# Weight sums of the mixers moved into the second gate/up loops, head sums and projection loads shifted, a second transpose bank

## The chip, the cores and the metric

The program runs on one core of a Trainium2 chip. Time is device time in microseconds of one execution. The core has engines that run side by side, each through its own list of instructions in order: TensorE (PE, the matmuls), VectorE (DVE), ScalarE (ACT), GpSimd (POOL), and SyncE (SP), which issues the DMA transfers. An instruction that waits holds up all those behind it on its engine.

## The reference

A decoder trunk of two layers on x of shape (1, 1024, 1024), in float32:

```python
for layer in range(2):
    h = h + 0.5 * rmsnorm(swiglu(rmsnorm(h, g0), w_gate, w_up, w_down), g1)     # FFN 0
    m = rmsnorm(h, mix_pre_g[layer])
    m = hybrid_mixer(m, ...) if layer == 0 else stick_breaking(m, ...)
    h = h + rmsnorm(m, mix_post_g[layer])
    h = h + 0.5 * rmsnorm(swiglu(rmsnorm(h, g2), w_gate, w_up, w_down), g3)     # FFN 1

def swiglu(x, wg, wu, wd):
    return (silu(x @ wg) * (x @ wu)) @ wd            # 1024 -> 1408 -> 1024
```

The hybrid mixer projects h once, gives the parts to four heads of differential softmax attention (the difference of two softmax maps, blocks of 128 queries) and four heads of gated linear attention (GLA, chunks of 64), and projects the joined heads with `w_out`. Stick breaking is causal attention with eight heads whose weights come from sums of log(1 − sigmoid), with its own `w_out`.

## The kernel before

**Products.** Every float32 product is made of three passes over a high and a low part (`mm3`, L280 to L284). A raw weight tile is split by a cast on ACT (L331) and a subtraction on VectorE (L332) into a tile `wq` (helper `split_w`); the other operand, `hl`, is split in L272 and L273. Large products are done by Strassen-like schemes, which need sums and differences of weight blocks and save matmuls.

**Raw weights.** All weights come from DRAM into the pool `rp`, whose slots (tag `raw`) hold 512 KB each. There are four, given out in turn. A new load goes into the slot whose turn it is, once the last reader of what lay there is through. Gate, up, block, head and projection tiles all share these four.

**FFN** (`ffn`, L585). The function `gu` has two loops over the 11 columns (of 128) of gate and up. The first loop (from L398) takes one gate tile per column and does two quarters of 12 matmuls each (bank `pa`). It runs first in the program for FFN 0 of layer 0, right after the start. The second loop (from L425) takes a gate and an up tile per column, and makes on POOL four subtractions of blocks, in place:

```python
gt(out=b11, in0=b12, in1=b11, op=ALU.subtract)   # L431
gt(out=t2, in0=b22, in1=b11, op=ALU.subtract)    # L432
gt(out=b12, in0=b22, in1=b12, op=ALU.subtract)   # L433
gt(out=b21, in0=b21, in1=t2, op=ALU.subtract)    # L434
```

Five quarters of 12 matmuls follow, in the order t2 (bank `pb`), b12 (`pc`), b11 (`pd`), b21 (`pc` again, added on top) and b22 (`pd` again). VectorE takes the partial results out: `ph<-pb` (L444), `c22<-pc` (L447), `c22<-pd` (L461), `c21<-pc` (L464), `c12<-pd` (L467), and multiplies (L468, L469). So the second use of `pc` can only begin when `c22<-pc` has read the first. The splits into `wq` are one column ahead of the matmuls. From column 6 on, two more operations on POOL (`down_sums`, L608 and L609) prepare the down projection, `down_strassen`.

**Weight sums of the mixers.** The value projections and the output projections of both mixers use block sums too (`Blocks.sums`, L75). One job loads four blocks of 256 KB into two raw slots (`rawd`, L60), makes four subtractions on POOL (L64), and stores two results of 512 KB to DRAM (`vsum` or `wsum`, L87), from where the projection loads them later. There are 16 jobs: four for the hybrid mixer's value projection, in the first loop of the first FFN; eight (its output projection, and the value projection of layer 1) in the diff heads, at query blocks 1, 4 and 6; four (output projection of layer 1) in stick-breaking heads 0 to 3, at block 6.

**Heads.** Both kinds of attention run through `heads` (L978): per step one block of 128 queries of one head: scores (bank `z`), weights, transposes of the weights into the bank `tps` (L971) and copies from it (`att`, L973), the product with v (`po`), and a normalisation for which POOL makes `rs` (L230) and VectorE `on` (L1150). `self.soon` holds functions that run one step later, `steps` a list of projection steps of which one runs per block; at block 2 the steps for the next head are added (`fill`). Each projection step list loads its raw weights (`rawt`, L875) and splits them at its first step. `put_o` (L1414) stores a finished head (`otd`), loads two stored heads back (`raws`), makes sums of them on POOL a step later (`out_sums`, L1440 to L1443) and stores these (`osum`, L1429).

**Order.** The functions are written out in one thread; a scheduler then orders instructions on each engine, on SP too, by when it expects operands. Instructions that are kept in program order stay where they were written against each other.

Of the kernel before, what the change touches and what calls it, by code (L numbers as in the profile page):

```python
# [19 lines left out]
P = 128  # L20
D = 1024
# [23 lines left out]

class Blocks:
# [18 lines left out]

    def b11(self, j):
        return self.load((j, 0))[:, 0]

    def b21(self, j):
        return self.load((j + self.KH, 0))[:, 0]  # L70

    def b22(self, j):
        return self.load((j + self.KH, 1))[:, 0]

    def sums(self, j, dst):  # L75
# [5 lines left out]
        def make():  # L81
# [15 lines left out]
class Trunk:  # L97
# [247 lines left out]
    def gu(self, cx, wg, wu, A, xn1, gname, gi, jobs):  # L345
# [52 lines left out]
        for c in range(NF):  # L398
# [26 lines left out]
        for c in range(NF):  # L425
# [8 lines left out]
            gt(out=b21, in0=b21, in1=t2, op=ALU.subtract)  # L434
            pb = self.acc.tile([P, TB], F32, name="pb", tag="acc")
# [34 lines left out]
            if c > NF // 2:  # L470
                self.down_sums(ph, c - 1 - NF // 2)
        tmp.close()
# [112 lines left out]
    def ffn(self, l, f, x0, xn1, hsrc, hdst, last):  # L585
# [5 lines left out]
        jobs = [(self.value_blocks(0), j, self.tv) for j in range(4)] if l + f == 0 else []  # L591
# [281 lines left out]
    def load_tile(self, w, c0, n=P):  # L873
        r = self.rp.tile([P, KD, P], F32, name="rawt", tag="raw")
        self.nc.sync.dma_start(out=r[:, :, :n], in_=w[:, c0:c0 + n].rearrange("(k p) m -> p k m", p=P))  # L875
        return r

    def split_tile(self, w, c0, n=P):
        nc = self.nc
        r = self.load_tile(w, c0, n)  # L880
        wh = self.wp.tile([P, KD, P], F32R, name="wh", tag="w")
        wl = self.wp.tile([P, KD, P], F32R, name="wl", tag="w")
        nc.scalar.copy(out=wh[:, :, :n], in_=r[:, :, :n])
        nc.vector.tensor_tensor(out=wl[:, :, :n], in0=r[:, :, :n], in1=wh[:, :, :n].bitcast(F32), op=ALU.subtract)
        return wh, wl

    def proj_steps(self, w, c0, X, dst):

        wt = []

        def step(tb, kh):
            if not wt:
                wt.extend(self.split_tile(w, c0))
# [8 lines left out]
        return [lambda tb=tb, kh=kh: step(tb, kh) for tb in range(2) for kh in range(2)]  # L902

    def halves_first(self, a, b):
        return a[:2] + b[:2] + a[2:] + b[2:]
# [746 lines left out]
```

## Time and profile before

| | us |
|---|---|
| median of 3 runs | 2520.13 (2518.27 to 2523.79) |
| the profiled execution | 2520.03 |
| its span, first to last instruction | 2518.3 |
| TensorE busy | 2367.1 |
| VectorE busy | 1905.4 |
| ScalarE busy | 1139.0 |
| GpSimd busy | 889.1 |

The mean granted clock of TensorE is 0.983. Times in the trace count from the start of the span. The stages that matter here: first gate/up loop of the first FFN from 16.7 to 103.6 us, its second loop up to some 250; GLA in 510 to 660; the diff heads in 675 to 900; the stick-breaking heads in 1700 to 2125. A row of a timeline gives start, duration, engine, line, operation, output and inputs, and in brackets how long the engine was idle before it and what it waited for. A row of a group gives count, busy time, mean of one in ns, and the idle time before with its causes.

### The profile page before, as it was taken

What the parts mean: (1) busy time and instruction counts of PE and PEld (TensorE: products, weight loads), DVE (VectorE), ACT (ScalarE), POOL (GpSimd) and SP (SyncE); (2) the same over time, 40 slices, a digit from 0 to 9 for tenths busy, and PEclk for the clock granted to TensorE, in tenths of its full rate; (3) what the DMA queues carried; (4) which work ended last, traced back from release to release, by engine and by line L of the source; (5) the groups of instructions that cost most, each with busy time, mean ns of one, the idle gap of its engine ahead of it and who ended that gap; (6) DMA issues with size and microseconds to landing.
All of it is one profiled execution on the core that took longest, in us unless ns stands there. A gap on an engine that the chain in (4) does not pass through costs nothing.

```text
span 2518.3 us, 32043 instructions
## 1 busy us (share of the span) xinstructions
PE 2367.1 (94%) x11165; PEld 1926.7 (77%) x11165; DVE 1905.4 (76%) x2884; ACT 1139.0 (45%) x2286; POOL 889.1 (35%) x756
## 2 busy tenths in 40 slices
PE   6999998998988999999989999999999989999998
PEld 4788777777776777788868888777888877788886
DVE  5867888387576877768888678985666678786798
ACT  5423456332465756423456224563333335652343
POOL 4345532024123111545532456301322340244554
PEclk9999999999999999999999999999999999999999
DMA  7422544514325354222652225546220136622255
GB/s 242 118 83 68 185 158 141 167 51 147 113 95 174 129 199 141 76 84 78 212 177 82 84 71 171 164 150 217 84 84 26 59 109 225 194 84 75 71 167 193
DMA packets 272506, 324.27 MB, mean 129 GB/s; under 512 B 13828, under 2 KB 190168, under 8 KB 272344
## 3 DMA queue, kind: packets, MB, share of 16 engines
q1 hardware_dynamic: 272344, 322.22, 40.2%
q8 instruction: 88, 1.44, 0.2%
q14 instruction: 74, 0.61, 0.1%
HBM read 256.11 MB, written 66.06 MB: 128 GB/s over the span
## 4 chain that ended last, share of the span: by engine, by line
PE 35%; DVE 12%; issue 10%; DMA 6%; POOL 5%; ACT 2%; SPq 0%; POOLq 0%; DVEq 0%; ACTq 0%
DVE hl L273 4%; PE pc L283 2%; PE pc L284 2%; PE pc L282 2%; PE pd L283 2%; PE pd L284 2%; PE pd L282 2%; PE pa L284 2%; PE pa L282 2%; PE pa L283 2%; DMA rawd<-in_ffn_w_down_dram 1%; POOL rs L230 1%; PE pb L283 1%; PE pb L282 1%; PE pb L284 1%
## 5 line engine op out<-in xcount | busy, mean ns | idle before, releaser
L331 ACT CAST wq<-rawt 128x512 fp32r<-128x512 f32 x264 | 162.7, 623 | 364.5 <-PE pc L284 170.4
L230 POOL TENSOR_TENSOR rs<-ms,nhalf 128x1 f32<-128x1 f32 (+1 forms) x136 | 104.3, 774 | 498.8 <-DVE ms L228 382.1
L332 DVE TENSOR_TENSOR wq<-rawt,wq 128x512 fp32r<-128x512 f32 x264 | 247.0, 941 | 35.0 <-ACT wq L331 29.4
L282 PE MATMUL pps<-hl,wh 128*128 128x512 f32 x512 | 209.2, 409 | 2.1 <-DVE q L921 2.1
L431 POOL TENSOR_TENSOR rawt<-rawt 128x512 f32<-128x512 f32 x44 | 73.2, 1664 | 373.6 <-DMA rawt<-in_ffn_w_up_dram 240.9
L284 PE MATMUL pps<-hl,wl 128*128 128x512 f32 x512 | 204.1, 399 | 0.0
L283 PE MATMUL pps<-hl,wh 128*128 128x512 f32 x512 | 203.8, 398 | 0.0
L272 ACT CAST hl<-rawd 128x512 fp32r<-128x512 f32 x192 | 117.9, 620 | 150.9 <-PE dc L284 21.6
L273 DVE TENSOR_TENSOR hl<-rawd,hl 128x512 fp32r<-128x512 f32 x192 | 156.4, 819 | 28.0 <-ACT hl L272 27.5
L282 PE MATMUL pa<-hl,wq 128*128 128x512 f32 x352 | 144.8, 411 | 14.7 <-ACT ph L404 8.1
L284 PE MATMUL pa<-hl,wq 128*128 128x512 f32 x352 | 142.8, 406 | 12.0 <-DVE wq L332 12.0
L64 POOL TENSOR_TENSOR rawd<-rawd 128x512 f32<-128x512 f32 x64 | 88.9, 1390 | 157.0 <-DMA rawd<-in_sb_w_out_dram 100.8
L283 PE MATMUL pa<-hl,wq 128*128 128x512 f32 x352 | 142.0, 403 | 0.0
L273 DVE TENSOR_TENSOR hl<-ph,hl 128x512 fp32r<-128x512 f32 x136 | 141.6, 1053 | 0.0
L282 PE MATMUL pc<-hl,wq 128*128 128x512 f32 x336 | 131.4, 391 | 3.4 <-DVE c L447 3.4
L284 PE MATMUL pc<-hl,wq 128*128 128x512 f32 x336 | 132.1, 393 | 0.0
L283 PE MATMUL pc<-hl,wq 128*128 128x512 f32 x336 | 132.1, 393 | 0.0
L283 PE MATMUL pd<-hl,wq 128*128 128x512 f32 x336 | 131.3, 391 | 0.0
L284 PE MATMUL pd<-hl,wq 128*128 128x512 f32 x336 | 131.2, 390 | 0.0
L282 PE MATMUL pd<-hl,wq 128*128 128x512 f32 x336 | 131.0, 390 | 0.0
L1042 DVE TENSOR_TENSOR_SCAN a<-a,zero 128x128 f32<-128x128 f32 (+3 forms) x64 | 92.6, 1447 | 50.6 <-POOL a L1039 50.0
L955 PE MATMUL z<-k,q 128*128 128x512 f32 (+2 forms) x480 | 115.9, 365 | 2.7 <-ACT e L1114 2.6
(346 smaller groups left out, 6831.1 us busy)
## 6 DMA issues: line engine op xcount, KB each, us to landing
rawt<-in_ffn_w_gate_dram SPq DMA_DIRECT2D x88, 512.0 KB, 4.0
rawd<-in_ffn_w_down_dram SPq DMA_DIRECT2D x60, 512.0 KB, 4.0
rawd<-in_ffn_w_down_dram SPq DMA_DIRECT2D x116, 256.0 KB, 2.8
rawt<-in_ffn_w_up_dram SPq DMA_DIRECT2D x44, 512.0 KB, 4.0
hres<-h SPq DMA_DIRECT2D x40, 512.0 KB, 2.8
h<-hres SPq DMA_DIRECT2D x40, 512.0 KB, 4.5
vsum<-rawd SPq DMA_DIRECT2D x16, 512.0 KB, 2.8
rawd<-vsum SPq DMA_DIRECT2D x32, 256.0 KB, 3.4
```

Source lines behind the costliest of these rows:

```text
L64: self.t.nc.gpsimd.tensor_tensor(out=out, in0=a, in1=b, op=ALU.subtract)
L230: nc.gpsimd.tensor_tensor(out=rs, in0=ms, in1=self.nhalf.to_broadcast([P, n]) if n > 1 else self.nhalf, op=ALU.pow)
L272: nc.scalar.copy(out=t[:, 0], in_=src)
L273: nc.vector.tensor_tensor(out=t[:, 1], in0=src, in1=t[:, 0].bitcast(F32), op=ALU.subtract)
L282: nc.tensor.matmul(ps, lhsT=ah, rhs=bh, start=first, stop=False, skip_group_check=more)
L283: nc.tensor.matmul(ps, lhsT=ah, rhs=bl, start=False, stop=False, skip_group_check=more)
L284: nc.tensor.matmul(ps, lhsT=al, rhs=bh, start=False, stop=last, skip_group_check=more)
L331: nc.scalar.copy(out=w[:, 0], in_=src)
L332: nc.vector.tensor_tensor(out=w[:, 1], in0=src, in1=w[:, 0].bitcast(F32), op=ALU.subtract)
L431: gt(out=b11, in0=b12, in1=b11, op=ALU.subtract)
L955: nc.tensor.matmul(z[:, :wide], lhsT=lhs[:, i * P:(i + 1) * P], rhs=rhs[:, c0:c0 + wide], start=j == 0, stop=j == len(passes) - 1 and not ...
L1042: nc.vector.tensor_tensor_scan(out=ra, data0=ra, data1=self.zero1.to_broadcast([P, n]), initial=1.0, op0=ALU.mult, op1=ALU.add)
```

## The change

1. No job runs in the first loop, the diff heads or the stick-breaking heads any more. All are in second gate/up loops: eight (value and output projection of layer 0) in FFN 0 of layer 0, in columns 0 to 7; four (value projection of layer 1) in FFN 1 of layer 0; four (output projection of layer 1) in FFN 0 of layer 1. A job's blocks are loaded at the end of a column's code, its sums come behind the next column's four subtractions, its stores at that column's end. Loads and stores of jobs are kept in program order.
2. `put_o`: sums one step later as before, the stores another step later, kept in program order; in layer 1 the head at hand is used as it lies, not loaded again.
3. Projections of the heads behind the first: raw weights are loaded at block 1 (kept in program order), split at block 2 by `prep`; of two step lists that are interleaved, the second is split with the first one's first step.
4. Diff heads 0 to 2 have two transpose banks and one bank for the projections' accumulators; for head 3 the banks are opened again as before (one and two).

```diff
 class Blocks:
     def load(self, *places):
         r = self.t.rp.tile([P, 2, TB], F32, name="rawd", tag="raw")
         for i, (k, c) in enumerate(places):
-            self.t.nc.sync.dma_start(out=r[:, i], in_=self.src(k, c))
+            self.t.tc.keep_in_program_order(self.t.nc.sync.dma_start(out=r[:, i], in_=self.src(k, c)))
...
             self.sub(b[:, 0], b[:, 0], b[:, 1])
+            return store
+
+        def store():
             for i, t in enumerate((r, b)):
-                self.t.nc.sync.dma_start(out=dst[j][:, i * D:(i + 1) * D], in_=t.rearrange("p c m -> p (c m)"))
+                self.t.tc.keep_in_program_order(self.t.nc.sync.dma_start(
+                    out=dst[j][:, i * D:(i + 1) * D], in_=t.rearrange("p c m -> p (c m)")))
...
@@ first loop of gu
                 combos(c - 4)
-            if sums:
-                sums.pop(0)()
-            if jobs:
-                B, j, dst = jobs.pop(0)
-                sums.append(B.sums(j, dst))
@@ second loop of gu
             gt(out=b21, in0=b21, in1=t2, op=ALU.subtract)
+            sums = [f() for f in sums]
...
                 self.down_sums(ph, c - 1 - NF // 2)
+            if sums:
+                sums.pop(0)()
+            if jobs:
+                B, j, dst = jobs.pop(0)
+                sums.append(B.sums(j, dst))
@@ ffn
-        jobs = [(self.value_blocks(0), j, self.tv) for j in range(4)] if l + f == 0 else []
+        jobs = []
+        if l + f == 0:
+            jobs += [(self.value_blocks(0), j, self.tv) for j in range(4)]
+            jobs += [(self.out_blocks(0), j, self.td) for j in range(4)]
+        elif f != l:
+            jobs += [(self.value_blocks(1), j, self.tv) if f else (self.out_blocks(1), j, self.td) for j in range(4)]
@@ proj_steps
+        raw = [self.load_tile(w, c0, pin=True)] if early else []
         wt = []
+        def prep():
+            wt.extend(self.split_tile(w, c0, raw))
@@ halves_first
-        return a[:2] + b[:2] + a[2:] + b[2:]
+        def first():
+            a[0]()
+            b.prep()
+        return Steps([first, a[1]] + b[:2] + a[2:] + b[2:], a.prep)
@@ heads
-            job = weights(h, i) if u < n else None
-            if job:
-                self.soon.append(job)
...
+            if u < n and i == 1:
+                nxt = fill(h)
             if u < n and i == 2:
-                steps += fill(h)
+                nxt.prep()
+                steps += nxt
@@ diff heads
-                self.open_mix(pd, 4, 1, 1)
+                self.open_mix(pd, 4, 2, 1)
...
                 def start(h):
+                    if h == 3:
+                        pd.close()
+                        self.mctx.close()
+                        self.open_mix(pd, 4, 1, 1)
...
-                def weights(h, i):
-                    if jobs and i in (1, 4, 6):
-                        B, j, dst = jobs.pop(0)
-                        return B.sums(j, dst)
@@ put_o
-            r, o = [self.rp.tile([P, S], F32, name="raws", tag="raw") for _ in range(2)]
-            for t, m in ((r, self.out_order(l)[j]), (o, k)):
-                self.nc.sync.dma_start(out=t, in_=self.ot[l][m])
+            pin = self.tc.keep_in_program_order
+            r = self.rp.tile([P, S], F32, name="raws", tag="raw")
+            pin(self.nc.sync.dma_start(out=r, in_=self.ot[l][self.out_order(l)[j]]))
+            o = ot
+            if l == 0:
+                o = self.rp.tile([P, S], F32, name="raws", tag="raw")
+                pin(self.nc.sync.dma_start(out=o, in_=self.ot[l][k]))
             def sums():
                 self.out_sums(r, o, o, self.nc.gpsimd.tensor_tensor)
+                return store
+            def store():
                 for i, t in enumerate((r, o)):
-                    self.nc.sync.dma_start(out=self.sd[j][:, i * S:(i + 1) * S], in_=t)
+                    pin(self.nc.sync.dma_start(out=self.sd[j][:, i * S:(i + 1) * S], in_=t))
```

The order of instructions at three places, before and after. First SP in the second loop of the first FFN; the numbers behind the names tell tiles apart. Before:

```order
L342 DMA rawt_1007<-in_ffn_w_gate_dram 128x8x128
L342 DMA rawt_1009<-in_ffn_w_up_dram 128x8x128
L342 DMA rawt_1105<-in_ffn_w_gate_dram 128x8x128
L342 DMA rawt_1107<-in_ffn_w_up_dram 128x8x128
L342 DMA rawt_1203<-in_ffn_w_gate_dram 128x8x128
L342 DMA rawt_1205<-in_ffn_w_up_dram 128x8x128
```

After:

```order
L68 DMA rawd_1069<-in_hyb_w_in_dram 128x512 x2
L68 DMA rawd_1072<-in_hyb_w_in_dram 128x512 x2
L345 DMA rawt_1075<-in_ffn_w_gate_dram 128x8x128
L345 DMA rawt_1077<-in_ffn_w_up_dram 128x8x128
L89 DMA vsum1_133<-rawd_1069 128x1024
L89 DMA vsum1_133<-rawd_1072 128x1024
L68 DMA rawd_1179<-in_hyb_w_in_dram 128x512 x2
L68 DMA rawd_1182<-in_hyb_w_in_dram 128x512 x2
L345 DMA rawt_1185<-in_ffn_w_gate_dram 128x8x128
L345 DMA rawt_1187<-in_ffn_w_up_dram 128x8x128
```

With four slots given out in turn, rawt_1185 and rawt_1187 take the places of rawt_1075 and rawt_1077, the column just ahead of them; before, rawt_1203 took the place of rawt_1007, two columns ahead.

Second, VectorE in the same loop, one column with the splits for the next. Before:

```order
L444 TENSOR_TENSOR ph_447<-pb,ph_447 128x512
L332 TENSOR_TENSOR wq<-rawt,wq 128x512
L447 TENSOR_TENSOR c_1246<-pc,ph_447 128x512
L332 TENSOR_TENSOR wq<-rawt,wq 128x512
L461 TENSOR_TENSOR c_1246<-pd,c_1246 128x512
L332 TENSOR_TENSOR wq<-rawt,wq 128x512
L464 TENSOR_TENSOR c_1263<-pc,ph_447 128x512
L332 TENSOR_TENSOR wq<-rawt,wq 128x512
L467 TENSOR_TENSOR c_1264<-pd,ph_447 128x512
L332 TENSOR_TENSOR wq<-t_1403,wq 128x512
L468 TENSOR_TENSOR ph_446<-ph_446,c_1264 128x512
L469 TENSOR_TENSOR ph_447<-c_1263,c_1246 128x512
```

After:

```order
L443 TENSOR_TENSOR ph_352<-pb,ph_352 128x512
L335 TENSOR_TENSOR wq<-t_1189,wq 128x512
L335 TENSOR_TENSOR wq<-rawt,wq 128x512
L446 TENSOR_TENSOR c_1122<-pc,ph_352 128x512
L335 TENSOR_TENSOR wq<-rawt,wq 128x512
L460 TENSOR_TENSOR c_1122<-pd,c_1122 128x512
L335 TENSOR_TENSOR wq<-rawt,wq 128x512
L463 TENSOR_TENSOR c_1139<-pc,ph_352 128x512
L335 TENSOR_TENSOR wq<-rawt,wq 128x512
L466 TENSOR_TENSOR c_1140<-pd,ph_352 128x512
L467 TENSOR_TENSOR ph_351<-ph_351,c_1140 128x512
L468 TENSOR_TENSOR ph_352<-c_1139,c_1122 128x512
```

The split of the next column's t2 moved from behind `c12<-pd` (two multiplications ahead of the next column) to behind the next column's `ph<-pb`, ahead of `c22<-pc`.

Third, POOL in the diff heads. Before:

```order
L64 TENSOR_TENSOR rawd<-rawd 128x512
L230 TENSOR_TENSOR rs<-ms,nhalf 128x1
L64 TENSOR_TENSOR rawd<-rawd 128x512 x2
L230 TENSOR_TENSOR rs<-ms,nhalf 128x1
L64 TENSOR_TENSOR rawd<-rawd 128x512 x6
L230 TENSOR_TENSOR rs<-ms,nhalf 128x1
L64 TENSOR_TENSOR rawd<-rawd 128x512 x3
L1440 TENSOR_TENSOR raws<-raws 128x512
L230 TENSOR_TENSOR rs<-ms,nhalf 128x1 x5
```

After:

```order
L233 TENSOR_TENSOR rs<-ms,nhalf 128x1 x7
L1468 TENSOR_TENSOR raws<-raws 128x512
L1469 TENSOR_TENSOR raws<-raws 128x512
L1470 TENSOR_TENSOR raws<-raws 128x512
L233 TENSOR_TENSOR rs<-ms,nhalf 128x1
```

The block subtractions (`rawd`) are gone from between the `rs`; those of the head sums (`raws`) stay.

More of the change, by code (lines that the diff above doesn't have):

```diff
@@ L43, in tile, with __init__ @@
         return self.pool().tile(shape, dtype, name=name, tag=self.tag)
+class Steps(list):
+    def __init__(self, steps, prep):
+        super().__init__(steps)
+        self.prep = prep
 class Blocks:
@@ L64, in sub @@
         self.t.nc.gpsimd.tensor_tensor(out=out, in0=a, in1=b, op=ALU.subtract)
[L66 to L73, printed above, removed]
     def sums(self, j, dst):
@@ L900, in step @@
                 dst(ps, slice(tb * TB, (tb + 1) * TB))
-        return [lambda tb=tb, kh=kh: step(tb, kh) for tb in range(2) for kh in range(2)]
+        return Steps([lambda tb=tb, kh=kh: step(tb, kh) for tb in range(2) for kh in range(2)], prep)
     def halves_first(self, a, b):
-        return a[:2] + b[:2] + a[2:] + b[2:]
+        def first():
+            a[0]()
+            b.prep()
+        return Steps([first, a[1]] + b[:2] + a[2:] + b[2:], a.prep)
     def scaled(self, t, scale):
@@ L976, in transposer, with heads @@
         return res, [lambda j0=j0: group(j0) for j0 in range(0, i + 1, 4)]
-    def heads(self, H, first, second, third, fill, start, weights, steps):
+    def heads(self, H, first, second, third, fill, start, steps):
         LAG = 2
@@ L1022, in heads @@
                 third(*done)
-        for step in steps + self.soon:
+        for step in steps:
             step()
+        while self.soon:
+            self.soon = [g for g in [f() for f in self.soon] if g]
     def sb_weights(self, q, k, i):
@@ L1087, in sb_mixer @@
             self.heads(8, lambda h, i: self.sb_weights(q[h], k[h], i), second, lambda h, i, r: None,
-                       lambda h: project(h + 1) if h < 7 else self.out_steps(1), start,
-                       lambda h, i: self.out_blocks(1).sums(h, self.td) if h < 4 and i == 6 else None, begin[5:])
+                       lambda h: project(h + 1) if h < 7 else self.out_steps(1), start, begin[5:])
             pd.close()
@@ L1406, in fill @@
                         return self.out_steps(0)
-                    return self.halves_first(q_diff(h + 1), k_diff(h + 1))
+                    return self.halves_first(q_diff(h + 1, True), k_diff(h + 1, True))
                 self.heads(4, lambda h, i: self.diff_weights(q[h], k[h], i, rcs),
                            lambda h, i, pts: self.diff_rows(rcs.pop(0), v[h // 2], (h % 2) * P, i, pts),
-                           third, fill, start, weights, begin[2:])
+                           third, fill, start, begin[2:])
                 pd.close()
@@ L1497, in out_steps @@
         self.begun = B, order, st
-        return [lambda tp=tp, ns=ns: step(tp, ns) for tp in range(2) for ns in ((0, 1), (2, 3), (4, 5), (6,))]
+        return Steps([lambda tp=tp, ns=ns: step(tp, ns) for tp in range(2) for ns in ((0, 1), (2, 3), (4, 5), (6,))],
+                     lambda: None)
     def mix_out(self, l, hsrc, hdst, gname, gi):
```

36 lines of the change are left out of this document (19 added, 17 removed).

## The prediction

> **What bounds the kernel now.** I read the page first (parts 1, 2 and 4), then windows by stage, then for the stages that the change touches the timelines of SP, POOL, VectorE and PE, the groups by form, and the waits.
>
> ```profile
> PE 2367.1 (94%) x11165; PEld 1926.7 (77%) x11165; DVE 1905.4 (76%) x2884; ACT 1139.0 (45%) x2286; POOL 889.1 (35%) x756
> 115.00:232.00 117.00, 117.00 (x512) 95.81 (x511) 81.18 (x105) 32.46 (x52) 56.93 (x39) 1.00 0.28 80
> 16.70:103.60 86.90, 71.63 (x297) 56.52 (x297) 64.85 (x84) 48.76 (x88) 33.56 (x26) 0.90 0.64 195
> 959.90:1029.90 70.00, 67.16 (x299) 54.77 (x298) 58.58 (x95) 47.06 (x88) 23.53 (x16) 0.96 0.32 98
> 510.00:660.00 150.00, 136.82 (x754) 109.40 (x752) 115.25 (x168) 41.22 (x97) 47.82 (x36) 0.99 0.35 120
> 675.00:900.00 225.00, 199.28 (x1074) 160.47 (x1074) 169.90 (x434) 143.74 (x404) 54.96 (x59) 0.98 0.38 129
> 1700.00:2125.00 425.00, 402.76 (x2211) 341.49 (x2210) 282.86 (x383) 163.99 (x340) 118.26 (x156) 0.98 0.35 113
> ```
>
> The first row is the page's, the others are windows: length, busy time and count of PE, PEld, DVE, ACT and POOL, the granted clock, the DMA share, GB/s. TensorE is the bound, with 151 us idle in the whole span. Where that idle time lies decides this case. The second gate/up loop of the first FFN (115 to 232) has none: PE 117.00 of 117.00 us at clock 1.00. The first loop of that FFN (16.7 to 103.6), where the value sums are made now, takes 86.9 us for 297 matmuls; the same loop of the next FFN takes 70.0 for 299. The GLA part (510 to 660) has 13.2 us of PE idle, the diff heads (675 to 900) 25.7, the stick-breaking heads (1700 to 2125) 22.2. So the change takes work out of stages where PE waits and puts it into the stage where PE does not wait at all.
>
> **The second loops: what the added sums do.** One column is 60 matmuls; 117.00 us over 512 is 0.2285 us each, so 13.7 us a column. Weights go through four raw slots. Now a column takes two of them and is loaded two columns ahead. In the changed order a job's two tiles take the other two, in eight columns of the first FFN and four each of the FFNs behind the hybrid mixer and ahead of the other one: 16 columns. There a column's weights can only go where the column just ahead of it lay, and that is free when its last quarter has been split. The rows of that handover now, from the timelines of DVE, SP and POOL:
>
> ```profile
> 115.64 0.69 DVE L464 TENSOR_TENSOR c<-pc,ph 128x512 f32<-128x512 f32 x1 [0.39 <-PE pc L284]
> 116.29 0.69 DVE L332 TENSOR_TENSOR wq<-rawt,wq 128x512 fp32r<-128x512 f32 x1
> 117.01 0.37 SPq L342 DMA_DIRECT2D rawt<-in_ffn_w_up_dram  x1
> 122.03 1.72 POOL L431 TENSOR_TENSOR rawt<-rawt 128x512 f32<-128x512 f32 x1 [7.34 <-DMA rawt<-in_ffn_w_up_dram]
> 125.08 1.75 POOL L433 TENSOR_TENSOR rawt<-rawt 128x512 f32<-128x512 f32 x1
> 130.82 0.37 SPq L342 DMA_DIRECT2D rawt<-in_ffn_w_up_dram  x1
> 135.43 1.31 POOL L431 TENSOR_TENSOR rawt<-rawt 128x512 f32<-128x512 f32 x1 [7.35 <-DMA rawt<-in_ffn_w_up_dram]
> 135.67 1.61 DVE L332 TENSOR_TENSOR wq<-rawt,wq 128x512 fp32r<-128x512 f32 x1
> 137.67 0.69 DVE L447 TENSOR_TENSOR c<-pc,ph 128x512 f32<-128x512 f32 x1 [0.39 <-PE pc L284]
> ```
>
> ```profile
> L332 DVE TENSOR_TENSOR wq<-rawt,wq 128x512 fp32r<-128x512 f32 x35 | 36.3, 1038 | 1.3
> L331 ACT CAST wq<-rawt 128x512 fp32r<-128x512 f32 x34 | 21.2, 622 | 73.3 <-PE pc L284 36.2 <-PE pb L284 19.8 <-PE pd L284 17.3
> L432 POOL TENSOR_TENSOR t<-rawt 128x512 f32<-128x512 f32 x8 | 12.7, 1583 | 0.6
> L433 POOL TENSOR_TENSOR rawt<-rawt 128x512 f32<-128x512 f32 x8 | 12.2, 1526 | 0.0
> L431 POOL TENSOR_TENSOR rawt<-rawt 128x512 f32<-128x512 f32 x8 | 10.8, 1353 | 55.3 <-DMA rawt<-in_ffn_w_up_dram 32.6 <-DVE ph L469 22.7
> L608 POOL TENSOR_TENSOR s<-ph,ph 128x512 f32<-128x512 f32 x4 | 5.6, 1402 | 4.4 <-DVE ph L469 4.4
> ```
>
> Today the wait of POOL for `up` ends early enough, because what is loaded at 117.01 belongs to the column after next. In the changed order of VectorE the splits of t2 and b12 of the next column stand ahead of this column's `c22<-pc`, and the second use of that pc bank by PE waits for `c22<-pc`. So the handover becomes a loop that runs once per column:
>
> - from `c21<-pc` to the issue of `up`: 115.64 to 117.01, 1.4 us;
> - issue to landing: 117.01 to 122.03 is 5.0, 130.82 to 135.43 is 4.6;
> - three subtractions on POOL: 1.35 + 1.58 + 1.53 = 4.5 by the groups; 122.03 to 126.83 is 4.8;
> - cast 0.62, split 1.04, `c22<-pc` 0.69: 2.4;
> - the twelve matmuls of pc again: 12 x 0.2285 = 2.7, and `c21<-pc` starts anew.
>
> Sum 15.6 to 16.3 us where the column needs 13.7: 1.9 to 2.6 us a column. On top come things that the trace does not show in this stage. POOL's work there goes from 0.49 of the time (56.93 of 117) by four more subtractions of about 1.4 to some 11.8 us of a column, so the b22 split, which now finds POOL idle (0.69), will find it busy: take the mean, 1.04, 0.35 more. And three times the bytes go past (1 MB of weights, 1 MB of blocks, 1 MB of stores), some beside `up`. From below that costs nothing; from above the landing comes later by half a store of the same size:
>
> ```profile
> vsum<-rawd SPq DMA_DIRECT2D x16, 512.0 KB, 2.8
> ```
>
> 1.4 us. I take 2.9 a column: 2.25, 0.35 and 0.3, near the lower end, since the DMA share is only 0.28 there now. 16 x 2.9 = 46. In columns 7 and 8 of the first FFN both down-sum operations come to stand ahead of the third subtraction: 2 x 2 x 1.40 = 5.6. Together **52 us lost**; at the ends 16 x 1.9 = 30 with the down sums, when they fit in a gap, at nothing, and 16 x 4.35 + 5.6 = 75.
>
> A rule that speaks against the change: the Trainium skill (SBUF — State Buffer, Who interferes with whom) says that a VectorE instruction with two SBUF inputs and a GpSimd one that reads SBUF exclude each other, and the later one blocks until the first ends. The trace agrees: the split that begins just behind a POOL subtraction takes 1.61 in place of 0.69, and `c22<-pc`, with one operand in PSUM, takes 0.69 while POOL runs. If by that rule both splits of the loop came to 1.61, the column would cost 0.57 + 0.57 more, 18 us in all, and the time would be 2544.
>
> **What the other stages get back.**
>
> First loop of the first FFN. It loses four jobs (16 subtractions, 16 loads, 8 stores). It becomes the loop of the other FFNs: 86.9 − 70.0 = **17 us** gained, 12 to 22, since the loop's first columns still begin beside the loading of x.
>
> ```profile
> PE pa L282 <- ACT wq L331: 6.5, 3, 3.3
> PE pa L284 <- DVE wq L332: 6.4, 3, 4.5
> PE lv L1210 <- DVE zq L1203: 7.0, 9, 2.6
> PE tps L971 <- DVE att L973: 8.0, 10, 1.9
> DVE on L1150 <- POOL rs L230: 13.0, 19, 1.6
> DVE k L921 <- ACT k L920: 9.2, 7, 2.5
> PE po L1082 <- DVE att L973: 7.6, 7, 2.6
> ```
>
> These are waits (total us, times, longest): two of the first loop, one of GLA, three of the diff heads, one of the stick-breaking heads. The first two, 12.9 us, are weights that come late, and they go.
>
> GLA. Out-block subtractions drift into it on POOL today. Of the 7.0 us at `lv` I take 5, with 0 and 10 as ends.
>
> Diff heads. POOL's `rs` waits behind block subtractions, VectorE's `on` waits for `rs`, and the copy of the transposed weights is queued behind `on`:
>
> ```profile
> 747.79 0.55 POOL L230 TENSOR_TENSOR rs<-ms,nhalf 128x1 f32<-128x1 f32 x1
> 748.37 0.41 DVE L1150 TENSOR_SCALAR on<-po,rs,rc 128x128 f32<-128x128 f32 x1 [1.59 <-POOL rs L230]
> ```
>
> 13.0 us in 19 waits. `rs` itself (0.55) stays, 10 of the 13 can go, and PE's 8.0 us at `tps` are part of the same. The second transpose bank works on the same waits. Gain **10**, 0 to 20. The bank comes from the projections: 12 evictions in heads 0 to 2. I cost that at nothing because a step of a projection comes once per query block, 225 / 32 = 7 us apart; without that cover it is 12 x 1.3 (9.2 / 7) = 16.
>
> Stick-breaking heads. Four jobs leave POOL, and the projection loads are issued two blocks sooner. Now they come late for heads 5 on, behind the head sums; from SP's timeline:
>
> ```profile
> 1927.83 41.13 SPq L1419 DMA_DIRECT2D otd<-ot  x2
> 1971.77 1.02 SPq L875 DMA_DIRECT2D rawt<-in_sb_w_qkv_dram  x2
> 2014.83 0.32 SPq L1419 DMA_DIRECT2D otd<-ot  x1
> 2018.27 1.01 SPq L875 DMA_DIRECT2D rawt<-in_sb_w_qkv_dram  x2
> 2060.83 0.32 SPq L1419 DMA_DIRECT2D otd<-ot  x1
> ```
>
> A head's store marks its end: 41.1 us from 1927.83 to 1968.6, then 46.2 and 46.0 for the two whose loads go at 1971.77 and 2018.27. Two heads by 5 us are 10, and half of the 7.6 us at `po` another 4: gain **14**, 5 to 22 (all its idle time). Storing the head sums a tile later and not reloading o cost and bring nothing beside this: they are DMA under a share of 0.35.
>
> **The sum**: 2520.0 (the profiled execution, 1.7 us over its span and 0.1 under the median) + 52 − 17 − 5 − 10 − 14 = **2526 us**.
>
> **Rivals.**
>
> *The weights still land in time* (the other side). If `c22<-pc` were not held up, because the next column's splits find their data ready, the loops stay at 13.7 us and the gains remain: 2520 − 46 = 2474. For it: 7.3 us of POOL idle ahead of each `L431` shows spare time. Against it: that spare time is counted from a load for the column after next, and the four slots no longer allow one.
>
> *The loop at its lower price*: 1.9 a column and no price for the down sums, 30 us: 2520 + 30 − 46 = 2504.
>
> *The clock drops after each stall.* In the stick-breaking stage a wait of 2.57 us is followed by matmuls of the same shape at 0.63 in place of 0.39:
>
> ```profile
> 1981.54 0.71 PE L1082 MATMUL po<-att,v 128*128 128x128 f32 x4 [2.57 <-DVE att L973]
> 1983.83 0.63 PE L282 MATMUL pps<-hl,wh 128*128 128x512 f32 x1
> ```
>
> A stall of 2.9 per column is of that size. If each of 16 is followed by some 3.4 us at 0.63 / 0.39, some 1.2 us each is lost, 19 us, less what the next stall then absorbs: 2545. Against it: PE's idle time then is 2.9 of 16.6, far from the whole. The Trainium skill (TensorE: Matmul & The Clock Gate, What's actually happening) wants at least one idle window of about 3.4 us before the clock falls; by it these stalls cost nothing more and the sum stays at 2526. The row above, slow after 2.57, goes against the page, so the rival keeps a chance.
>
> *The mixers' waits are their own.* If att and zq are late by VectorE's own work (169.90 of 225 in the diff heads) and not by POOL's subtractions, and the loads gain nothing, only the first loop's 17 and some 3 us come back: 2520 + 52 − 20 = 2552.
>
> SP's order (stores of a job, then loads of the next, then gate and up) is no rival: a job's sums end about 12 us after its column's `up` has landed, the store adds 2.8, and the gate load queued behind is due a column and a half after that landing, 20 us.
>
> **How the numbers follow.** The forecast 0.44, with its own range 2512 to 2541; weights in time 0.17; lower price 0.14; clock or splits at the dear end 0.14; mixers' waits their own 0.11. This kernel's measurement can tell about 0.2%, 5 us, from no change. Faster than 2515: 0.17 + 0.14 + 0.03 of the forecast = 0.34. Within 5 us: 0.17, all from the forecast. Slower than 2525: 0.24 + 0.14 + 0.11 = 0.49. The range 2484 to 2555 leaves out most of the case with weights in time, and the far end of the last.
>
> **What would show it.** In the second loops of the first FFN and of the two beside the mixers: a column of 16 to 17 us over eight and four columns, 13.7 in those behind; PE at pc waiting for `c22<-pc`; VectorE's t2 split waiting for POOL's subtractions, and POOL for `up`. First loop of the first FFN near 70 us. In the diff heads the wait of `on` for `rs` at 3 us or less; stick-breaking heads of 41 us up to the last. I am wrong if PE is still busy without a gap in those second loops, if POOL there waits for block loads and not for `up`, or if the diff and stick-breaking heads stay at 225 and 425 us.

## The result

The changed kernel takes 2555.1 us (median of 4 runs, 2550.3 to 2559.1), 34 us more than before; the ratio is 1.0135, with a 95% interval of 1.0113 to 1.0157. The forecast was 2526 us, slower, with a range of 2484 to 2555. The sign came out, the size was well short: 6 us forecast, 34 measured, at the very end of the range.

The span of the profiled execution went from 2518.3 to 2548.6 us. Cut at the first and the last `ph<-pb` of each second gate/up loop, the 30 us lie here (us):

| stretch | before | after | difference | forecast |
|---|---|---|---|---|
| start, first loop of the first FFN | 110.1 | 88.9 | −21.2 | −17 |
| second loop, first FFN, 8 jobs | 135.2 | 174.2 | +39.0 | |
| to the next second loop: GLA, diff heads | 792.4 | 779.5 | −12.9 | −15 |
| second loop behind the hybrid mixer, 4 jobs | 134.7 | 153.9 | +19.1 | |
| to the next | 207.2 | 205.6 | −1.6 | 0 |
| second loop ahead of stick breaking, 4 jobs | 136.1 | 152.7 | +16.6 | |
| to the next: stick-breaking heads | 737.7 | 727.3 | −10.5 | −14 |
| last second loop, no job | 134.7 | 134.7 | 0 | 0 |
| the rest | 130.1 | 131.8 | +1.7 | 0 |
| the three loops with jobs | 406.0 | 480.8 | +74.7 | +52 |
| everything else | 2112.3 | 2067.8 | −44.5 | −46 |

The windows of the three loops that get jobs, before (first three rows) and in the changed kernel (next three), and of the changed kernel's first gate/up loop (length, busy time and count of PE, PEld, DVE, ACT, POOL, granted clock, DMA share, GB/s):

```profile
110.10:245.30 135.20, 134.66 (x588) 109.99 (x587) 94.32 (x122) 37.74 (x61) 64.02 (x44) 1.00 0.26 75
1037.70:1172.40 134.70, 133.29 (x582) 108.85 (x581) 93.50 (x122) 37.69 (x61) 65.31 (x45) 1.00 0.28 79
1379.60:1515.70 136.10, 136.10 (x596) 111.45 (x595) 95.24 (x122) 38.33 (x62) 64.89 (x45) 1.00 0.27 77
88.90:263.10 174.20, 150.59 (x603) 120.01 (x602) 98.69 (x124) 38.74 (x64) 111.49 (x77) 0.92 0.49 158
1042.60:1196.50 153.90, 139.03 (x585) 112.40 (x584) 100.44 (x124) 39.18 (x64) 88.59 (x61) 0.96 0.41 126
1402.10:1554.80 152.70, 142.88 (x603) 115.44 (x602) 99.29 (x123) 39.18 (x64) 88.70 (x61) 0.97 0.40 126
16.60:84.00 67.40, 63.60 (x289) 51.73 (x290) 57.32 (x82) 46.84 (x85) 14.53 (x12) 1.00 0.41 120
```

In the changed kernel's first loop with jobs PE waits for 174.2 − 150.6 = 23.6 us, where before it waited for 0.5. But its matmuls themselves also take longer, at a clock of 0.92.

The counts show one thing more. The cuts lie at an instruction of VectorE, and PE does not stand at the same matmul there before and after: the three windows hold 1766 matmuls before and 1791 after, though the whole kernel has 11165 in both. At 0.229 us each the 25 more are 6 us, work that moved over the cuts and is no loss. 15 of them, 3.4 us, come from the start, whose gain is so 17.8 us and not 21.2; seven come from the stretch behind the hybrid mixer's loop and are its 1.6 us. So the first loop's 39 us are 23 of waiting, 12.5 of slow matmuls and 3.4 of moved work, and the 74.7 us of the three loops are 46 of waiting, 23 of slow matmuls and 6 of moved work. By this count the three loops lose 69 us, and everything else gains 39, not 44.5.

The waits of PE in each of the three loops:

```profile
PE pc L285 <- DVE c L446: 23.6, 8, 4.6
PE pc L285 <- DVE c L446: 14.9, 4, 8.6
PE pc L285 <- DVE c L446: 9.8, 4, 4.5
```

There is only one: `pc` for `c22<-pc`, once in each column with a job. One turn of the loop behind it, from the timelines of DVE, SP and POOL, and PE at its end:

```profile
103.78 0.69 DVE L463 TENSOR_TENSOR c<-pc,ph 128x512 f32<-128x512 f32 x1 [2.39 <-PE pc L287]
104.43 0.69 DVE L335 TENSOR_TENSOR wq<-rawt,wq 128x512 fp32r<-128x512 f32 x1
105.16 0.38 SPq L345 DMA_DIRECT2D rawt<-in_ffn_w_up_dram  x1
109.37 1.30 POOL L429 TENSOR_TENSOR rawt<-rawt 128x512 f32<-128x512 f32 x1 [5.47 <-DMA rawt<-in_ffn_w_up_dram]
111.99 1.28 POOL L431 TENSOR_TENSOR rawt<-rawt 128x512 f32<-128x512 f32 x1
112.72 1.10 DVE L335 TENSOR_TENSOR wq<-t,wq 128x512 fp32r<-128x512 f32 x1 [2.74 <-ACT wq L334]
113.96 1.57 DVE L335 TENSOR_TENSOR wq<-rawt,wq 128x512 fp32r<-128x512 f32 x1
115.45 0.68 DVE L446 TENSOR_TENSOR c<-pc,ph 128x512 f32<-128x512 f32 x1
116.28 0.47 PE L285 MATMUL pc<-hl,wq 128*128 128x512 f32 x1 [1.49 <-DVE c L446]
119.29 0.69 DVE L463 TENSOR_TENSOR c<-pc,ph 128x512 f32<-128x512 f32 x1 [0.38 <-PE pc L287]
```

From `c21<-pc` at 103.78 to the next at 119.29 are 15.5 us; the forecast's list gave 15.6 to 16.3. Issue after 1.4, landing after 4.2, three subtractions in 3.9, the splits and `c22<-pc` 2.9 up to 116.1, and the twelve matmuls. VectorE sat idle for 2.74 us ahead of the t2 split, with `c22<-pc` queued behind it.

What the list did not have is the clock. The columns from one `ph<-pb` to the next:

```profile
88.90:109.30 20.40, 15.84 (x61) 12.52 (x60) 9.96 (x14) 3.63 (x6) 11.64 (x8) 0.83 0.62 201
109.30:124.80 15.50, 14.01 (x61) 11.19 (x60) 10.11 (x13) 3.64 (x6) 12.17 (x8) 1.00 0.55 178
124.80:143.20 18.40, 15.68 (x62) 12.37 (x61) 10.09 (x13) 3.63 (x6) 11.69 (x8) 0.91 0.58 189
```

and PE's own rows in the third of them:

```profile
133.01 0.47 PE L285 MATMUL pc<-hl,wq 128*128 128x512 f32 x1 [2.72 <-DVE c L446]
133.80 0.63 PE L285 MATMUL pc<-hl,wq 128*128 128x512 f32 x1
134.23 0.63 PE L286 MATMUL pc<-hl,wq 128*128 128x512 f32 x1
```

The column that waits 1.49 us runs at 1.00 and takes 15.5; the one that waits 2.72 has matmuls of 0.63 behind the wait, one every 0.43 us in place of 0.23, and takes 18.4. Of the 16 waits the ten of 1.89 us and more have such matmuls behind them, the six of up to 1.74 us do not. The slow matmuls are those of pc, which belong to the loop, so the loop gets longer by them too. And the first column of each loop costs 9 us, not 2.9 (20.4 against 11.0 before): its wait of 4.56 us comes because column 1 can only be loaded once column 0 has been split, at the loop's start.

### The profile page after: what moved, and what is told of

It is laid out like the page before. It is cut to its first block, busy times and chain, and to the rows that moved or that the text cites. A ratio compares the mean times of both kernels' runs of the same rounds, so it can differ in the third digit from the quotient of the medians.

```text
span 2548.6 us, 32007 instructions
## 1 busy us (share of the span) xinstructions
PE 2371.3 (93%) x11165; PEld 1928.9 (76%) x11165; DVE 1888.0 (74%) x2884; ACT 1136.9 (45%) x2286; POOL 883.9 (35%) x756
## 5 line engine op out<-in xcount | busy, mean ns | idle before, releaser
L285 PE MATMUL pc<-hl,wq 128*128 128x512 f32 x336 | 140.3, 418 | 49.6 <-DVE c L446 49.6
L285 PE MATMUL pa<-hl,wq 128*128 128x512 f32 x352 | 141.1, 401 | 9.7 <-ACT ph L407 9.6
L287 PE MATMUL pa<-hl,wq 128*128 128x512 f32 x352 | 138.9, 395 | 6.5 <-DVE wq L335 6.4
L286 PE MATMUL pc<-hl,wq 128*128 128x512 f32 x336 | 139.4, 415 | 0.0
L286 PE MATMUL pa<-hl,wq 128*128 128x512 f32 x352 | 138.9, 395 | 0.0
L287 PE MATMUL pc<-hl,wq 128*128 128x512 f32 x336 | 138.8, 413 | 0.0
L1065 POOL TENSOR_SCALAR_AFFINE_SELECT a<-a 128x128 f32<-128x128 f32 x64 | 20.3, 318 | 329.3 <-ACT a L1061 319.9
L286 PE MATMUL pd<-hl,wq 128*128 128x512 f32 x336 | 131.8, 392 | 0.0
```

What stands on the lines that cost most here:

```text
L285: nc.tensor.matmul(ps, lhsT=ah, rhs=bh, start=first, stop=False, skip_group_check=more)
L286: nc.tensor.matmul(ps, lhsT=ah, rhs=bl, start=False, stop=False, skip_group_check=more)
L287: nc.tensor.matmul(ps, lhsT=al, rhs=bh, start=False, stop=last, skip_group_check=more)
L1065: nc.gpsimd.affine_select(out=t[:, n - P:n], in_=t[:, n - P:n], pattern=[[-1, P]], compare_op=ALU.is_ge, fill=fill_with, base=-1, channel_ ...
```

## The experiments

### The jobs alone, and everything but the jobs

The first kernel is the changed one without its parts 2 to 4: `put_o`, `proj_steps`, `halves_first`, `fill` and the banks as before. The second is the reverse: parts 2 to 4, with `Blocks.sums` and the three places of the jobs as before.

```diff
-                self.open_mix(pd, 4, 2, 1)
+                self.open_mix(pd, 4, 1, 1)
...
-                return self.halves_first(q_diff(h + 1, True), k_diff(h + 1, True))
+                return self.halves_first(q_diff(h + 1), k_diff(h + 1))
```

> Only part 1 of the change (jobs in the second loops, their loads and stores in program order); head sums, projection loads and banks as before. In the changed kernel the second loops lost 74.7 us against before, the first loop with the start won 21, the stretch of the hybrid mixer 13 and that of the stick-breaking heads 10. If the mixers won because the jobs left them: same as the changed kernel, about 2555 us (2550 to 2560). If the other three parts won it: 2521 + 75 - 21 = 2575 us.

> Only parts 2 to 4 of the change (head sums, projection loads, banks); all jobs where they were before. If the mixers won because the jobs left them: 2521 us, no difference from before. If parts 2 to 4 won it: 2521 - 23 = 2498 us. Second loops 135 us each by both.

The jobs alone: 2540.5 us, ratio 1.0076 (1.0051 to 1.0101). Second loops +40, +17 and +17, as in the whole change; the start −21; GLA and diff heads −22.9, where the whole change has −12.9; stick-breaking heads −9.2. Parts 2 to 4 alone: 2525.4 us, ratio 1.0026 (1.0010 to 1.0043). The first lies below both its expected times, the second a little above the one for no difference. So the mixers win because the jobs leave them, and win more than the whole change shows; parts 2 to 4 together cost 5 us by themselves and 14.6 beside the moved jobs.

### The banks as before

```diff
-                self.open_mix(pd, 4, 2, 1)
+                self.open_mix(pd, 4, 1, 1)
...
-                    if h == 3:
-                        pd.close()
-                        self.mctx.close()
-                        self.open_mix(pd, 4, 1, 1)
```

> The changed kernel with the diff heads' banks as before (one for transposes, two for the projections' accumulators), everything else as changed. Moving the jobs alone measured 2540.5 us, 14.6 less than the whole change, and in the changed kernel PE waits 7.4 us in the diff heads at po for VectorE's on, and 4.3 us at z for the eviction of k: waits that neither the kernel before nor that with the jobs alone has. If the banks make them: about 2541 us (2536 to 2545), and po<-on is gone. If the earlier projection loads and splits or the head sums make them: 2551 or more.

2532.9 us (2530.3 to 2535.7), 22.2 below the whole change: below the range that I gave, since the projection loads and head sums are worth something, 7.6 us against the jobs alone. The banks cost 22. With them, in the diff heads of the changed kernel, PE waits (first two rows) and VectorE waits (last two) like this:

```profile
PE po L1170 <- DVE on L1175: 7.4, 8, 1.6
PE z L978 <- ACT k L961: 4.3, 3, 2.0
DVE k L944 <- ACT k L943: 9.4, 6, 2.5
DVE q L944 <- ACT q L943: 8.6, 4, 4.0
```

Evictions of the projections (`k`, `q`) hold up VectorE for 18.0 us there; with the banks as before its wait for `k` is 3.1. Which of the two banks does it is settled in the last experiment.

### The order of the splits

```diff
-            self.quarter(pb, self.split_w(t2), S[2], True, True)
+            self.quarter(pb, self.split_w(t2, behind), S[2], True, True)
...
-            self.quarter(pc, self.split_w(b12), S[3], True, True)
+            self.quarter(pc, self.split_w(b12, behind), S[3], True, True)
...
-            tt(out=c22, in0=pc, in1=u2, op=ALU.add)
+            behind = tt(out=c22, in0=pc, in1=u2, op=ALU.add)
```

`split_w` queues its VectorE instruction behind the one given, with no wait for it to end.

> The changed kernel with one thing added: in the second gate/up loops the VectorE splits of the next column's t2 and b12 are queued behind this column's c22<-pc. Slots, loads, sums and stores stay. Theory 1 (the loss is the order: PE waits for c22<-pc only because it stands behind splits whose data are late): the columns with jobs go back from 15.5 to 20 us to 13.8, the three loops to about 135 us, PE there is busy without gaps, and the time is 2555 - 75 = 2480 us (2472 to 2492). Theory 2 (with one column ahead the weights are late whatever the order): PE's wait moves from c22<-pc to the splits themselves (pb or pc <- wq), the columns stay above 15 us, time 2535 or more.

2561.1 us (2554.3 to 2566.1): nothing gained. PE's wait moved to the next read, `c22<-pd`, as nine waits of about the same sum, because the splits then stood ahead of that:

```profile
PE pd L285 <- DVE c L464: 23.0, 9, 5.2
```

In the last second loop, which has no job, the order alone cost 5 us (140.0 against 134.7). So the trial did not part the theories, and it was repeated on the jobs alone, with the splits of t2, b12 and b11 behind `c22<-pd`, behind both reads:

```diff
-                tt(out=c22, in0=pd, in1=c22, op=ALU.add)
+                read = tt(out=c22, in0=pd, in1=c22, op=ALU.add)
+                behind = read if jobs else None
```

> Part 1 of the change alone (2540.5 us), and in the columns with jobs the splits of the next column's t2, b12 and b11 stand behind this column's second read of pd's first product (c22<-pd), so behind both reads that PE waits for. In the earlier trial with t2 and b12 behind c22<-pc alone, PE's wait moved to c22<-pd, which had come to stand behind three splits. Theory 1 (the loss is the order, the weights come early enough): second loops 135 to 138 us each, PE's wait for c22 gone, 2540 - 66 to - 74 = 2466 to 2474 us, faster than before by 2%. Theory 2 (one column ahead is too late whatever the order): PE waits for wq instead, columns of 15.5 us and more, 2520 us or more.

2525.5 us, ratio 1.0022 (1.0010 to 1.0035); 15 us better than the jobs alone, but far from 2470. The second loops still cost +28, +15 and +14. The first column is down from 21.0 to 16.5 us, but the columns with a job take 16.3 to 18.2. PE still waits for `c22<-pc`, 17.0 us in the first loop, and hardly for `wq`, which theory 2 had expected. The loop that sets the columns no longer passes through PE (timelines of DVE, SP and POOL):

```profile
111.91 1.11 DVE L335 TENSOR_TENSOR wq<-t,wq 128x512 fp32r<-128x512 f32 x1 [3.21 <-ACT wq L334]
113.16 4.97 DVE L335 TENSOR_TENSOR wq<-rawt,wq 128x512 fp32r<-128x512 f32 x3
118.66 1.18 DVE L335 TENSOR_TENSOR wq<-rawt,wq 128x512 fp32r<-128x512 f32 x1
119.87 0.38 SPq L348 DMA_DIRECT2D rawt<-in_ffn_w_up_dram  x1
125.56 1.29 POOL L433 TENSOR_TENSOR rawt<-rawt 128x512 f32<-128x512 f32 x1 [4.58 <-DMA rawt<-in_ffn_w_up_dram]
128.91 1.11 DVE L335 TENSOR_TENSOR wq<-t,wq 128x512 fp32r<-128x512 f32 x1 [4.57 <-ACT wq L334]
```

t2 split to t2 split is 17.0 us, without a matmul in it: five splits, three of them 1.66 us each beside POOL's job (0.69 before, with POOL idle), the load of 5.7, two subtractions and a cast. The theory that the order alone makes the loss has fallen. With one column ahead the loop through the slots is longer than 13.7 us in either order. In this order the slowed splits have a part in that: the five take 7.3 us, and at 0.69 each they would take 3.5 and leave a turn of some 13.2 us. That is an estimate; this order was not run without POOL's subtractions.

The same with parts 2 and 3 of the change:

> The whole change with the banks as before and the order of splits as in the run with jobs and order. If the earlier projection loads and the moved head sums bring something beside the jobs: 2 to 10 us below that run. If they bring nothing or cost: within 3 us of it, or above.

2518.6 us, ratio 0.9991 (0.9974 to 1.0008): 7 us below the run without them, so the projection loads and head sums bring some 7 us here as they did above.

### Without POOL's subtractions

```diff
-            self.sub(r[:, 0], r[:, 1], r[:, 0])
-            self.sub(r[:, 1], b[:, 1], r[:, 1])
-            self.sub(b[:, 1], b[:, 1], r[:, 0])
-            self.sub(b[:, 0], b[:, 0], b[:, 1])
             return store
```

> The changed kernel without the four subtractions of each job: blocks are loaded into the two slots and stored again as they are, so the value and output projections of the mixers are computed from wrong sums. Slots, DMA and order stay, POOL has 6 us a column less. If slots and order make the loss, the loop through VectorE, SP, DMA and POOL stays at 15 to 15.5 us at full clock, PE still waits for c22<-pc, and the time is 2545 to 2555 us. If POOL's work (its own time, or its blocking of VectorE's splits) makes it: columns near 13.8 us and about 2490 us.

One run: 2535.9 us, 19 below the changed kernel, and below the 2545 to 2555 expected from slots and order, though nearer to that than to 2490. The second loops still cost +34.5, +15.3 and +10.7, 60.5 of the 74.7. The turn of the loop at full clock is 15.7 us, as it was with the subtractions, and PE waits in the first of the loops like this:

```profile
PE pc L281 <- DVE c L442: 21.4, 8, 4.3
```

So in this order the loop is as long without POOL's subtractions; slots, DMA and order are all kept here, and this run does not part them. POOL's work adds 14 us over the three loops; two thirds of that are waits (PE's wait for `c22<-pc` is 38.6 us in the three, 48.3 in the changed kernel), the rest lies in the time of the matmuls.

### PE's wait filled with matmuls

```diff
...
                 w4, w3 = self.split_w(b21), self.split_w(b22)
+                pin = self.tc.keep_in_program_order if jobs else None
+                if jobs:
+                    pj = self.acc.tile([P, TB], F32, name="pj", tag="acc")
+                    for k in range(8):
+                        pin(nc.tensor.matmul(pj, lhsT=w2[:, 0, k % 4], rhs=S[1][k % 4][:, 0], start=k == 0,
+                                             stop=k == 7))
...
```

> The changed kernel, with eight more matmuls (1.8 us, into a bank that nobody reads) ahead of the second use of pc in the columns with jobs, where PE waits 1.5 to 4.6 us. They add work and take nothing out of the loop through VectorE, SP, DMA and POOL, which at full clock is 15.5 us long. If the clock falls because of PE's waits (rows of 0.83 to 0.91 in the long columns, 1.00 in those of 15.5): most columns come to 15.5 to 16 us at clock 1.00, and the time falls by 16 to 28 us to about 2532. If the long columns come from the loads and not from the clock: no faster than 2555, up to 2585 with the added work.

2550.6 us (2546.7 to 2554.5): 4.5 below the changed kernel, with ranges that overlap, and not 2532. Columns of that kernel:

```profile
121.20:138.00 16.80, 15.78 (x69) 12.64 (x68) 10.07 (x12) 3.63 (x6) 12.08 (x9) 1.00 0.59 189
138.00:157.50 19.50, 17.47 (x69) 13.91 (x69) 10.09 (x12) 3.64 (x6) 13.69 (x10) 0.91 0.52 168
```

Where the filling left about 1 us of wait, the clock stayed at 1.00 and the column at 16.8 (before it 18.4 at 0.91). But `up` landed up to 6.7 us after its issue where it took 4.2 to 5.7, 14.5 us of waits were left in the first loop (23.6 before), and the added matmuls, 15 us there, ate what was won. That the clock goes with the waits is borne out by the columns (1.00 with a wait of 1.02 us, 0.91 with one of 2.03); the gain that I expected is not.

### A job in every other column

Banks as before. Jobs only at columns 1, 3, 5 and 7, four per loop; the four for layer 0's output projection go back to the diff heads.

```diff
-            if jobs:
+            if jobs and c % 2:
                 B, j, dst = jobs.pop(0)
                 sums.append(B.sums(j, dst))
...
-            jobs += [(self.out_blocks(0), j, self.td) for j in range(4)]
...
+                def weights(h, i):
+                    return (lambda: self.out_blocks(0).sums(h, self.td)) if i == 4 else None
```

> Banks as before. Jobs only in columns 1, 3, 5 and 7 of the three second loops; the four of layer 0's output projection go back to the diff heads (one per head, at block 4). So no two columns in a row have to take the place of the column just ahead, and column 0 takes no place from column 1. Theory 2 (the loop through the slots, 15.5 us without and 17 us with the order changed, is longer than a column of 13.7, and every column has to go through it): with a free column between, at most the stall of c22<-pc of 1.5 to 2 us is left once per job, PE waits 20 us in all over the three loops, no half clock, second loops 137 to 145 each, time 2470 to 2490 us. If what hurts is the load of the jobs on POOL and DMA at all: columns 1, 3, 5, 7 and their followers still take 3 to 6 us more per job, 2500 us or more.

2515.0 us, ratio 0.9975 (0.9959 to 0.9992), not the 2470 to 2490 of theory 2: by the number it is the other side, 2500 or more, and 3 to 4 us a job. Columns behind a job take 16 to 18 us, the last of them 20 to 21, those between 13 to 13.8. The first, which now has no job, takes 11 to 12.8, so its 9 us were the job's. The loops cost +17, +15 and +12. One `c22<-pc` wait per job stays, and in the first loop it is

```profile
PE pc L285 <- DVE c L446: 10.6, 4, 4.7
```

2.6 us each on the mean, more than I expected, and long enough for the clock: the column of 18.0 us around the first of them, a wait of 2.37, has 0.91.

Then the same with the splits of the column behind a job queued behind `c22<-pd`:

```diff
-                tt(out=c22, in0=pd, in1=c22, op=ALU.add)
+                read = tt(out=c22, in0=pd, in1=c22, op=ALU.add)
+                behind = read if jobs and c % 2 else None
```

> The same, and in the columns with a job the splits of the next column's t2, b12 and b11 stand behind c22<-pd. With a free column between, the loop through the slots has 27.5 us for two columns and should fit; the order then takes away the rest of PE's wait: second loops 135 to 137 us each, PE there without gaps, 5 to 20 us below the run without the order, 2462 to 2475 us. If the splits (1.6 us each beside POOL's subtractions) come too late for pb and pc: PE waits for wq there, and it is no faster than the run without.

2477.1 us (2476.2 to 2485.4), ratio 0.9840 (0.9818 to 0.9863): 44 us faster than the kernel before, 78 faster than the changed one, two us above the range expected. The first loop, and its waits:

```profile
89.50:230.20 140.70, 137.06 (x595) 111.12 (x595) 100.71 (x122) 37.62 (x62) 89.42 (x61) 1.00 0.43 133
PE pc L285 <- DVE c L450: 2.8, 2, 1.9
PE pc L285 <- ACT wq L334: 0.9, 1, 0.9
```

POOL is as busy as in the changed kernel's other loops (89 us), 133 GB/s go past, and PE waits 3.6 us at clock 1.00. A free column between two jobs gives the loop 27.4 us, and the order keeps it off PE. Each loop costs 5 us still. Two of them hold the same four jobs as in the changed kernel, where they cost 19 and 17, so it is not the load of the jobs as such that hurts, as the run without the order seemed to say.

### Which bank

On the fastest kernel, the change's banks again, and then the bank taken from the projections given to `po` in place of the transposes.

```diff
-                self.open_mix(pd, 4, 1, 1)
+                self.open_mix(pd, 4, 2, 1)       # the other kernel: 4, 1, 2
...
+                    if h == 3:
+                        pd.close()
+                        self.mctx.close()
+                        self.open_mix(pd, 4, 1, 1)
```

> The run with jobs in every other column and the order (2477 us) with the change's banks in diff heads 0 to 2: two for transposes, one for the projections' accumulators, opened again at head 3. In the changed kernel the banks cost 22 us (2555 against 2533 with the banks as before). The same here by both theories on its cause: 2490 to 2500 us, head 0 some 12 us longer.

> The same, but the bank taken from the projections' accumulators goes to po, and the transposes keep their one. Theory A (the one accumulator bank makes it: each projection step waits until VectorE and ScalarE have taken out the last): 2490 to 2500 us as with the second transpose bank, VectorE's waits for k and q on ACT as there (18 us in the changed kernel, 3 for k with the banks as before). Theory B (the second transpose bank makes it, since PE then runs ahead with transposes and VectorE's order changes): 2477 us or a little less.

2503.6 us with the second transpose bank, 26.5 more and a little above what was expected; 2514.4 with the second `po` bank, 37 more. Theory A holds, by more than its range: it is the accumulator bank that is missed, and the second transpose bank gives 11 back against giving it to `po`. Opening the banks again at head 3 is not the cause: of the 22 us that the second transpose bank costs between the first two loops with jobs, 18 are spent by the end of head 1, 14 of them in head 0 (from SP's head stores, 77.8 us in place of 63.4). Why head 0 pays most was not followed. PE's waits in the diff heads of the last kernel, whose profiled execution is its slowest of ten (2525.7 us), name the bank:

```profile
PE pps L285 <- ACT k L965: 12.4, 3, 6.6
PE pps L285 <- DVE q L948: 4.1, 3, 1.5
```

A projection step (`pps`) waits for the eviction of the one before. The fastest kernel has no such wait among its longest. With the second transpose bank the loss shows in another place: PE waits 7.7 us at `po` for `on` and 4.3 at `z` for `k`, and only 0.9 at `pps`.

## Why the prediction was right in sign and short in size

**The second loops.** The mechanism was the right one: slots, one column ahead, `c22<-pc` behind the next column's splits, 15.5 us measured for a turn where the list gave 15.6 to 16.3, and three subtractions of 6.7 us with both down sums in place of 3.9, as priced. The term that was mis-sized is the sum of it, 52 us forecast, 74.7 measured, and 69 without the work that moved over the cuts. Its waits came to 46 us. 23 are the clock, which stood among the rivals at 19 us, with a chance of 0.14 that it shared with dear splits, and should have stood in the sum. That 19 and 23 lie close is partly luck: ten of the 16 waits were followed by slow matmuls, not all, but each lost more than the 1.2 us that I took. I had compared the durations, 0.63 and 0.39, which overlap; by the starts, 0.43 and 0.23 us apart, 3.4 us of them lose 1.6, and behind the longer waits there were more of them. The row that I quoted (a wait of 2.57 us, matmuls of 0.63 behind it) was the better guide than the argument against it, that PE's idle share would be small. In the second gate/up loops of the changed kernel and of the runs, every wait of 3 us or more had slow matmuls behind it, none of up to 1.77 had, and between 1.78 and 2.79 both occur, so the length alone does not decide. The Trainium skill (TensorE: Matmul & The Clock Gate, What's actually happening) asks for an idle window of about 3.4 us; the trace disagrees.

**The first column.** Priced like the others at 2.9 us, it cost 9 in each of the three loops, 27 of the 74.7, so the waits of the other columns came out below the forecast and the near match of 46 with 52 is not one column by column. The list began with a loop that already turns; how it starts was not looked at.

**POOL and the port.** Splits beside POOL's jobs took 1.57 where the forecast had 1.04, but the b22 split, taken at 1.04, found POOL idle (0.69). The two miss in opposite directions. (POOL's busy time in a column, put at 11.8, is 12.3 by its own terms; 12.2 was measured.) The rule of the Trainium skill on the shared port (SBUF — State Buffer, Who interferes with whom) agrees with the splits of 1.66 us in the run whose loop has no matmul; in the changed kernel only one of the loop's two splits came near 1.61 (1.57, the other 1.10), and the loss over 52 us came from elsewhere.

**The start.** 17.8 us gained for 17, without the matmuls that moved over the cut. The first loop runs at 1.00 now, 0.90 before; the loop that I took as its model ran at 0.96.

**The mixers.** −12.9 for −15 and −10.5 for −14 look like near hits and are not. The jobs' leaving was worth more than I took (the jobs alone gain 22.9 in GLA and diff heads, and with the projection loads and head sums 30.1), and the exchange of banks, counted on the side of the gains with the lost accumulator bank at nothing, cost 22 us of the whole time. The step that failed there is the cover: "a step of a projection comes once per query block". The price without cover, 16, was the nearer one. POOL's part was overrated too: `on` still waits 7.1 us for `rs` in the changed diff heads where I gave 3 at most.

**Projection loads in the stick-breaking heads.** Heads of 41 us up to the last were expected. SP's timeline of the changed kernel:

```profile
1958.46 0.53 SPq L1440 DMA_DIRECT2D otd<-ot  x1
1999.42 0.34 SPq L1440 DMA_DIRECT2D otd<-ot  x1
2048.15 0.34 SPq L1440 DMA_DIRECT2D otd<-ot  x1
2090.89 0.32 SPq L1440 DMA_DIRECT2D otd<-ot  x1
```

41.0, then 48.7 and 42.7: one of the two late heads was mended in part, the other became later. Together they take 91.4 us where they took 92.2, so the 10 us priced for them did not come. Parts 2 to 4 alone have the same pattern (49.2 and 42.8), and the jobs alone gain 9.2 of the stretch's 10.5: that gain is the jobs' leaving, and that it lies near the forecast is luck. What holds the late head up was not followed.

**The rivals.** Weights still in time (0.17): refuted by 16 waits. The lower price: the loop's waits alone were already above it. The mixers' own waits: no, the jobs alone gain there. SP's order, called no rival, holds nothing up in the turn shown: `up` is issued at 105.16, at the end of the split that frees its slot (104.43 + 0.69).

## What to carry to other kernels

Work put into a stage where the bound engine never waits is not free because another engine has time there: ask which buffers it takes, how far ahead that leaves the loads, and whether the whole way from one release to the next (issue, landing, every engine's step, in each engine's order) still fits into one turn. If it does not, a free turn between two such jobs and reads queued ahead of the next turn's splits can do it, and neither did it alone here. And a stall long enough to lower the clock is to be priced with the slow matmuls behind it.

## What was not expected of the hardware

A wait of PE of 1.9 to 2.8 us can be followed by some 3.5 us of matmuls of 0.63 in place of 0.39 us, which start 0.43 us apart in place of 0.23; in the three loops this made 23 of 75 us. And `up` takes longer to land the closer it is issued behind `gate`. SP's and POOL's timelines of the changed kernel:

```profile
101.42 0.38 SPq L345 DMA_DIRECT2D rawt<-in_ffn_w_gate_dram  x1
105.16 0.38 SPq L345 DMA_DIRECT2D rawt<-in_ffn_w_up_dram  x1
...
118.94 0.38 SPq L345 DMA_DIRECT2D rawt<-in_ffn_w_gate_dram  x1
120.73 0.38 SPq L345 DMA_DIRECT2D rawt<-in_ffn_w_up_dram  x1
126.13 1.29 POOL L429 TENSOR_TENSOR rawt<-rawt 128x512 f32<-128x512 f32 x1 [4.28 <-DMA rawt<-in_ffn_w_up_dram]
```

With 3.7 us between the two issues it is 4.2 (to 109.37, above), with 1.8 it is 5.4: 1.2 us more for 2 us less between them.
